# Attention logits of two groups in one call, on 64-row tiles, with a bias tile in place of two extra rows

## The chip, the cores and the metric

The kernel runs on one core of a Trainium2 chip. The time is the device time of one execution in microseconds; several executions of the kernel before are summed up by their median. TensorE (PE) multiplies, VectorE (DVE), ScalarE (ACT) and GpSimd (POOL) work on elements, SyncE (SP) issues DMAs; each engine works its own instructions off in the order in which they stand.

## The reference

256 tokens, d_model 1024, two layers. Each layer is a SwiGLU FFN (width 2816), a token mixer and another SwiGLU FFN, all with RMSNorm before and after. The first layer's mixer is an RG-LRU; the second's is an attention of 16 heads of 64 with a forget gate, and that is where the change lies. Keys, values and the cumulative sum `c` of the forget gate's logarithm are computed once from the stream after the first layer:

```python
log_f = jax.nn.log_sigmoid(hn @ w_f + b_f)
c = jnp.cumsum(log_f, axis=1).transpose(0, 2, 1)            # heads x tokens
...
q = (xq @ w_q).reshape(Bn, S, N_HEADS, HEAD_DIM).transpose(0, 2, 1, 3) * (HEAD_DIM ** -0.5)
for blk in range(S // 128):                                  # two blocks of 128 queries
    logits = einsum('bhqd,bhkd->bhqk', q[:, :, q0:end], k[:, :, :end])
    logits = logits + c[:, :, q0:end, None] - c[:, :, None, :end]
    logits = where(kpos[None, :] <= qpos[:, None], logits, -inf)
    p = softmax(logits, axis=-1)
    outs.append(einsum('bhqk,bhkd->bhqd', p, v[:, :, :end]))
return concatenate(outs) @ w_o
```

Everything is float32.

## The kernel before

*Products.* Each large product is made of three matmuls of 128x512 (L183 to L185): weights and activations are split into a high part (`whi`, `xhi`) and a low part (`wlo`, `xlo`), and high x high, low x high and high x low are summed in PSUM. Weights stream from HBM on SP's queue into five `raw` buffers; ACT rounds each to `whi` (L173), DVE subtracts it to `wlo` (L177), and nine buffers of each lie between the splits and PE.

*Order of the work.* The kernel keeps a list of items, each one a piece of weight with the work that uses it, once for token half t=0 (tokens 0 to 127) and once for t=1. `slot` does one item for one half. PE's order is written out by hand; what ACT and DVE do is put in order by a scheduler, which lets steps marked `high_priority` go first, and `keep_in_program_order` fixes the order of single instructions. `defer(n, f)` issues `f` after n further slots, `ahead(i, f)` issues it with the preparation of item i. In the attention the order stands in a string, `ATT_ORDER`: `0` and `1` are the next item for that half (first the q projections, then the output projection's eight items, which accumulate over `oh`, `ol`), and `l`, `n`, `t`, `v` with a half are the next group's logits, norm, turn (transposes) and values.

*Attention.* A group is four heads at t=0 (128 keys) and two heads at t=1 (256 keys), so 512 logits in a row, one PSUM bank; there are four groups and eight. Keys and queries are held transposed, `kT` and `qT`, one head in 66 partitions: 64 of the head, and two rows that add c: q has c and -1 there, k has 1 and c with its sign, so a matmul over 66 rows gives the logit with both terms. The two rows of q come by four POOL DMAs (L947, L948), c's row of k by one per half (L994). `heads_T` scales a product's 512 columns (L954, DVE), turns them by four transposes (L959), and copies the even heads by ACT (L962) and the odd ones by DVE (L963). `running` makes c by fp32 matmuls with a triangular matrix (L991, L992).

For each group, `logits` does one matmul per head into a PSUM bank (L1063; the `gt` banks, two of them), adds the causal mask to the last block of keys in PSUM (L1064, DVE), takes the row maxima, negated (L1066, DVE), and one exp per head from PSUM with the sum accumulated beside it (L1071, ACT). `norm` multiplies by the reciprocals of the sums (L1077, L1078, DVE). `turn` does four transposes and a copy (L1084; L1086, ACT). `values` multiplies with v in pairs of heads on two halves of the columns (L1098); after eight heads the result is split into `oh` (L1104, ACT) and `ol` (L1105, DVE), which the output projection reads.

Just ahead of the attention lies the last FFN ("ffn3" in the notes on the list), whose up items end with `prod` (L510) after `sil` (L498, ACT) and whose transposes (L525) read a reloaded `prr`. The RMSNorm's reciprocal root is computed on POOL (L198, L200).

Of the kernel before, what the change touches and what calls it, by code (L numbers as in the profile page):

```python
# [16 lines left out]
P = 128  # L17
# [9 lines left out]
HA = HD + 2  # L27
# [17 lines left out]
def trunk_kernel(ctx: ExitStack, tc: tile.TileContext, A: dict, out: bass.AP):  # L45
# [8 lines left out]
    psum = ctx.enter_context(tc.tile_pool(name="psum", bufs=1, space=bass.MemoryType.PSUM))  # L54

# [862 lines left out]
    def kv_tiles():  # L918
        lp = ctx.enter_context(tc.tile_pool(name="kv", bufs=1, reuse_waits="tile"))
        kv["kT"] = lp.tile([HA, NH, S], F32, name="kT")  # L920
        kv["v"] = [lp.tile([P, D], F32, name=f"v{t}") for t in range(2)]

        kv["lf"] = [lp.tile([P, NH + 8], F32, name=f"lf{t}")[:, :NH] for t in range(2)]
        kv["c"] = [lp.tile([NH, P], F32, name=f"c{t}") for t in range(2)]
        kv["bfb"] = lp.tile([P, NH], F32, name="bfb")
        for n in ("triu", "mone", "cmask"):
            kv[n] = lp.tile([P, P], F32, name=n)

    def kv_constants():

        keep = tc.keep_in_program_order
        triu, cm = kv["triu"], kv["cmask"]
        keep(nc.gpsimd.dma_start(kv["bfb"], A["b_fgate"].partition_broadcast(P)))
        keep(nc.gpsimd.memset(triu, -1.0))
        keep(nc.gpsimd.affine_select(out=triu, in_=triu, compare_op=ALU.is_ge, fill=0.0, base=0,
                                     pattern=[[1, P]], channel_multiplier=-1))
        keep(nc.gpsimd.memset(kv["mone"], -1.0))
        keep(nc.gpsimd.memset(cm, 0.0))
        keep(nc.gpsimd.affine_select(out=cm, in_=cm, compare_op=ALU.is_ge, fill=NEG, base=0,
                                     pattern=[[-1, P]], channel_multiplier=1))  # L940
        keep(nc.gpsimd.memset(kv["kT"][HD:HA, :, :], 1.0))

    def att_rows():

        tc.keep_in_program_order(nc.scalar.activation(warm, mhalf, AF.Exp))
        for t in range(2):
            tc.keep_in_program_order(nc.gpsimd.dma_start(att["q"][t][HD:HD + 1, :, :], kv["c"][t]))  # L947
            tc.keep_in_program_order(nc.gpsimd.dma_start(att["q"][t][HD + 1:HA, :, :], kv["mone"][:NH, :]))  # L948

    def heads_T(pool, ps, t, n, scale, dst):  # L950

        tok = pool.tile([P, 512], F32, tag="prod", name=nm("htok"), bufs=2)
# [3 lines left out]
        def turn():  # L956
# [3 lines left out]
            to = dst[:HD, 8 * n:8 * n + 8, :].rearrange("p (a two) b -> p a two b", two=2)  # L960
            with tc.high_priority():
                nc.scalar.activation(to[:, :, 0, :], tp[:HD, :].rearrange("p (a b) -> p a b", a=4), AF.Copy)  # L962
                nc.vector.tensor_copy(to[:, :, 1, :], tp[HD:, :].rearrange("p (a b) -> p a b", a=4))  # L963
        defer(2, turn)

    def post_k(n):
        return lambda t, ps: heads_T(pools["f"], ps, t, n, 1.0, kv["kT"][:, :, t * P:(t + 1) * P])
# [20 lines left out]
    def running(t):  # L988
        pc = gtbank()
        if t == 1:  # L990
            nc.tensor.matmul(pc[:NH, :P], kv["lf"][0], kv["mone"], start=True, stop=False)  # L991
        nc.tensor.matmul(pc[:NH, :P], kv["lf"][t], kv["triu"], start=t == 0, stop=True)  # L992
        nc.vector.tensor_copy(kv["c"][t], pc[:NH, :P])
        nc.gpsimd.dma_start(kv["kT"][HD + 1:HA, :, t * P:(t + 1) * P], kv["c"][t])  # L994

# [41 lines left out]
    n_ffn3 = len(items)  # L1037

# [5 lines left out]
    def att_tiles():  # L1044
        ap = pools["a"]
        att["q"] = [ap.tile([HA, NH, P], F32, name=f"qT{t}") for t in range(2)]
# [3 lines left out]
    def attention(t):  # L1050
# [4 lines left out]
        mask = kv["cmask"].unsqueeze(1).to_broadcast([P, per, P])  # L1055
# [3 lines left out]
        def logits(hg):  # L1059
            hds = range(hg * per, (hg + 1) * per)  # L1060
            ps = gtbank().rearrange("p (a b) -> p a b", a=per)
            for j, hd in enumerate(hds):
                nc.tensor.matmul(ps[:, j, :], att["q"][t][:, hd, :], kv["kT"][:, hd, :nk * P], start=True, stop=True)  # L1063
            nc.vector.tensor_tensor(ps[:, :, t * P:], ps[:, :, t * P:], mask, ALU.add)  # L1064
            mx = spool.tile([P, 4], F32, tag="mx", name=nm("mx"))
            nc.vector.tensor_reduce(mx[:, :per], ps, AX.X, ALU.max, negate=True)  # L1066
            if hds[0] % 8 == 0:
# [292 lines left out]
```

## Time and profile before

Three executions took 987.85 to 989.92 us, median 988.57. The profiled execution took 987.51 us, of which 985.8 are the span that the trace covers, at a granted TensorE clock of 0.998.

| what | before |
|---|---|
| PE busy | 978.0 us, 99% |
| DVE busy | 616.6 us, 63% |
| ACT busy | 530.1 us, 54% |
| POOL busy | 47.2 us, 5% |
| logits matmuls (L1063) | 64 records, from 734.7 to 776.3 us |
| masks (L1064) and maxima (L1066) | 12 and 12 on DVE, mean 0.51 and 0.68 us |
| exps (L1071) | 32 on ACT, and 32 reads of the accumulator at 0.20 us |
| DMA, mean | 193 GB/s |

A row of the groups' view names the line, engine, operation, the tile written and those read, the shapes and the count; then come the busy time in us and the mean of one in ns, and behind the next bar the idle time of the engine just before, with what ended it. An fp32 matmul has two records. In the order of one engine, the first number is the start and the second the length; lengths of neighbours on PE overlap, so the distance from start to start is what a step costs. A row of windows gives the stretch and its length, the busy time of PE, PEld (weight loads), DVE, ACT and POOL with counts, the granted clock, the DMA share and GB/s.

### The profile page before, as it was taken

To read this page: it belongs to the slowest core of one execution; us is meant where nothing else is said; L and a number is where in the kernel's file an instruction comes from. 1 tells how busy PE (TensorE), PEld (TensorE's weight loads), DVE (VectorE), ACT (ScalarE), POOL (GpSimd) and SP (SyncE) were. 2 spreads that over 40 slices of the span, in tenths; PEclk is the share of its full clock that TensorE was granted. 3 is DMA by queue.
4 is the path that set the end of the run, shared out by engine and by line. 5 is a ranking of instruction groups with operands and counts; after the bars stand their busy time and mean duration, and the time that the engine had idled before them with its cause. 6 is when DMAs were issued, how large, how long until landed. Compare 5 with 4: busy or idle time off the path is not lost.

```text
span 985.8 us, 13028 instructions
## 1 busy us (share of the span) xinstructions
PE 978.0 (99%) x4777; PEld 813.4 (83%) x4777; DVE 616.6 (63%) x791; ACT 530.1 (54%) x753; POOL 47.2 (5%) x92
## 2 busy tenths in 40 slices
PE   9999999999999999999999999999999999999997
PEld 6888888898978888888898888888888788888886
DVE  6666554678997555554686655554488876555542
ACT  7545443568986544443564444544366755444431
POOL 2400000100003000000100000000020000000000
PEclk9999999999999999999999999999999999999999
DMA  8787766565346877666567676665552467776631
GB/s 292 263 266 249 222 210 192 158 192 162 117 126 198 241 211 212 217 207 188 131 203 242 186 220 213 214 213 185 190 173 64 123 210 235 213 213 212 205 117 43
DMA packets 99558, 190.45 MB, mean 193 GB/s; under 512 B 12734, under 2 KB 32614, under 8 KB 99494
## 3 DMA queue, kind: packets, MB, share of 16 engines
q1 hardware_dynamic: 98054, 188.95, 61.3%
q8 instruction: 38, 0.62, 0.3%
q10 hardware_dynamic: 608, 0.53, 0.2%
q0 software_dynamic: 832, 0.12, 0.1%
q14 instruction: 26, 0.21, 0.1%
HBM read 176.95 MB, written 1.05 MB: 181 GB/s over the span
## 4 chain that ended last, share of the span: by engine, by line
PE 98%; issue 1%; DVE 1%; ACT 0%; POOL 0%; POOLq 0%; DVEq 0%; ACTq 0%
PE mm L183 29%; PE mm L185 29%; PE mm L184 28%; PE gt L761 2%; PE tr L525 1%; PE mm L1195 1%; PE gt L1063 1%; PE mm L190 1%; PE mm L191 1%; PE mm L192 1%; PE mm L1098 1%; PE tr L1084 1%; PE gt L214 1%; PE tr L127 0%; PE tr L959 0%
## 5 line engine op out<-in xcount | busy, mean ns | idle before, releaser
L177 DVE TENSOR_TENSOR wlo<-raw,whi 128x1024 fp32r<-128x1024 f32 (+5 forms) x329 | 395.3, 1207 | 268.3 <-ACT whi L173 266.1
L173 ACT ACTIVATE whi<-raw 128x1024 fp32r<-128x1024 f32 (+5 forms) x329 | 341.9, 1046 | 314.8 <-PE mm L185 260.2
L183 PE MATMUL mm<-whi,xhi 128*128 128x512 f32 (+1 forms) x768 | 301.2, 392 | 0.0
L185 PE MATMUL mm<-whi,xlo 128*128 128x512 f32 (+1 forms) x768 | 298.2, 388 | 0.3 <-DVE xlo L228 0.3
L184 PE MATMUL mm<-wlo,xhi 128*128 128x512 f32 (+1 forms) x768 | 297.9, 388 | 0.0
L185 PEld LDWEIGHTS mm<-whi,xlo 128*128 128x128 f32 x768 | 144.2, 188 | 30.7 <-DVE xlo L228 0.7
L183 PEld LDWEIGHTS mm<-whi,xhi 128*128 128x128 f32 x768 | 144.2, 188 | 29.4 <-issue 1.3
L184 PEld LDWEIGHTS mm<-wlo,xhi 128*128 128x128 f32 x768 | 144.3, 188 | 28.2 <-DVE wlo L177 0.3
L183 PE MATMUL mm<-whi,hhi 128*128 128x512 f32 x352 | 137.9, 392 | 0.0
L185 PE MATMUL mm<-whi,hlo 128*128 128x512 f32 x352 | 137.1, 389 | 0.0
L184 PE MATMUL mm<-wlo,hhi 128*128 128x512 f32 x352 | 137.0, 389 | 0.0
L185 PEld LDWEIGHTS mm<-whi,hlo 128*128 128x128 f32 x352 | 66.1, 188 | 13.9
L184 PEld LDWEIGHTS mm<-wlo,hhi 128*128 128x128 f32 x352 | 66.1, 188 | 13.3
L183 PEld LDWEIGHTS mm<-whi,hhi 128*128 128x128 f32 x352 | 66.1, 188 | 13.3
L510 DVE SCALAR_TENSOR_TENSOR prod<-mm,rstd,sil 128x512 f32<-128x512 f32 (+1 forms) x48 | 33.8, 705 | 35.2 <-PE mm L185 31.1
L498 ACT ACTIVATE sil<-mm,rstd 128x512 f32<-128x512 f32 (+1 forms) x48 | 31.2, 651 | 38.7 <-PE mm L185 34.2
L198 POOL TENSOR_SCALAR nv<-ss 128x1 f32<-128x1 f32 x22 | 9.6, 435 | 716.3 <-ACT junk L205 716.3
L529 ACT ACTIVATE hhi<-tr 128x512 fp32r<-128x512 f32 (+1 forms) x48 | 24.8, 558 | 13.8 <-PE tr L525 13.8
L205 ACT ACTIVATE junk<-mm 128x512 bf16<-128x512 f32 x24 | 14.3, 595 | 32.7 <-PE mm L185 32.6
L272 DVE TENSOR_TENSOR t<-mm,gb 128x512 f32<-128x512 f32 x24 | 16.1, 685 | 24.7 <-ACT junk L205 24.6
L530 DVE TENSOR_TENSOR hlo<-tr,hhi 128x512 fp32r<-128x512 f32 (+1 forms) x48 | 29.2, 640 | 2.6 <-ACT hhi L529 2.6
L183 PE MATMUL mm<-whi,zhi 128*128 128x340 f32 (+2 forms) x80 | 28.2, 353 | 0.0
(196 smaller groups left out, 885.8 us busy)
## 6 DMA issues: line engine op xcount, KB each, us to landing
raw<-in_ffn_w_down_dram SPq DMA_DIRECT2D x88, 512.0 KB
raw<-in_ffn_w_up_dram SPq DMA_DIRECT2D x80, 512.0 KB
raw<-in_ffn_w_gate_dram SPq DMA_DIRECT2D x78, 512.0 KB
prr<-prod SPq DMA_DIRECT2D x40, 256.0 KB
raw<-in_rg_w_in_dram SPq DMA_DIRECT2D x10, 504.0 KB
raw<-in_rg_w_out_dram SPq DMA_DIRECT2D x10, 504.0 KB
raw<-in_ffn_w_gate_dram SPq DMA_DIRECT2D x19, 256.0 KB
raw<-in_ffn_w_up_dram SPq DMA_DIRECT2D x16, 256.0 KB
```

The costliest lines, as they stand in the source:

```text
L173: up = nc.scalar.activation(hi[:parts, c:c + m], rawv[:, c:c + m], AF.Copy)
L177: nc.vector.tensor_tensor(lo[:parts, c:c + m], rawv[:, c:c + m], hi[:parts, c:c + m].bitcast(F32), ALU.subtract)
L183: nc.tensor.matmul(ps, xh, wh, start=first, stop=False)
L184: nc.tensor.matmul(ps, xh, wl, start=False, stop=False)
L185: nc.tensor.matmul(ps, xl, wh, start=False, stop=last)
L205: nc.scalar.activation(junk[:, :src.shape[1]], src, AF.Square, scale=f, accum_out=acc)
L272: nc.vector.tensor_tensor(t1[n], pf[n], gb[:, n * 512:(n + 1) * 512], ALU.mult)
L498: nc.scalar.activation(s[:, :nn], ps, AF.Silu, scale=rs[t][:, 0:1])
L510: nc.vector.scalar_tensor_tensor(pr[:, :nn], ps, rs[t][:, 0:1], s, ALU.mult, ALU.mult)
L529: nc.scalar.activation(hv, tp[:, :nn], AF.Copy)
L530: nc.vector.tensor_tensor(lv, tp[:, :nn], hv.bitcast(F32), ALU.subtract)
L761: nc.tensor.matmul(ps[j][:w, g * S:(g + 1) * S], wv[rows, o:o + w], xc[rows, k, :], start=start, stop=stop, skip_group_check=True)
```

## The change

The two extra rows go. `kT` and `qT` now hold two heads in 128 partitions, the even head in rows 0 to 63 and the odd one in rows 64 to 127, so `heads_T` needs one ACT copy of 128x512 and no DVE copy. The causal mask and the keys' part of c become a bias: for t=0 a tile `bias0` (128 queries x 16 heads x 128 keys), for t=1 a table `bias1` of 128 x 16 x 256, made in DRAM and read into SBUF as one DMA of 2 MB ahead of the attention. Both are filled by POOL DMAs that give each partition c's rows, and by a select on POOL that puts the mask's value where the key is later than the query; `bias1`'s right half goes in four parts through tiles of the `sil` buffers during the FFN before. `running` also makes `cq`, c with queries on the partitions, by more matmuls with 16 columns.

One call of `logits` now does two groups. Its heads alternate between two `gt` banks and between the upper and the lower 64 rows of PE. For each head one DVE operation (tensor_tensor_reduce, in the program two instructions: the operation and the reading of its accumulator) takes the logit, adds the bias, negates, writes to SBUF and gives the row's minimum. Two small DVE operations for each group add and subtract `cq`, so that the minimum is rounded as it would be with the query's c in it, and the exps read SBUF with scale -1. The call of the second group does nothing on its own. `ATT_ORDER` is rewritten: the calls of `l` that do the work, and the turns and values, stand at other places among the items.

```diff
--- before.py
+++ after.py
@@ -917,39 +917,63 @@
 
     def kv_tiles():
         lp = ctx.enter_context(tc.tile_pool(name="kv", bufs=1, reuse_waits="tile"))
-        kv["kT"] = lp.tile([HA, NH, S], F32, name="kT")
+        kv["kT"] = lp.tile([P, NH // 2, S], F32, name="kT")
         kv["v"] = [lp.tile([P, D], F32, name=f"v{t}") for t in range(2)]
 
         kv["lf"] = [lp.tile([P, NH + 8], F32, name=f"lf{t}")[:, :NH] for t in range(2)]
-        kv["c"] = [lp.tile([NH, P], F32, name=f"c{t}") for t in range(2)]
+        kv["cq"] = [lp.tile([P, NH], F32, name=f"cq{t}") for t in range(2)]
         kv["bfb"] = lp.tile([P, NH], F32, name="bfb")
-        for n in ("triu", "mone", "cmask"):
-            kv[n] = lp.tile([P, P], F32, name=n)
+        kv["triu"] = lp.tile([P, P], F32, name="triu")
+        kv["one"] = lp.tile([P, 32], F32, name="one")[:, :1]
+        kv["bias0"] = lp.tile([P, NH, P], F32, name="bias0")
+        kv["rows"] = dram.tile([NH, S], F32, name="crows")
+        kv["bias1"] = dram.tile([P, NH, S], F32, name="bias1d")
 
     def kv_constants():
 
         keep = tc.keep_in_program_order
-        triu, cm = kv["triu"], kv["cmask"]
+        triu = kv["triu"]
         keep(nc.gpsimd.dma_start(kv["bfb"], A["b_fgate"].partition_broadcast(P)))
-        keep(nc.gpsimd.memset(triu, -1.0))
+        keep(nc.gpsimd.memset(triu, 1.0))
         keep(nc.gpsimd.affine_select(out=triu, in_=triu, compare_op=ALU.is_ge, fill=0.0, base=0,
                                      pattern=[[1, P]], channel_multiplier=-1))
-        keep(nc.gpsimd.memset(kv["mone"], -1.0))
-        keep(nc.gpsimd.memset(cm, 0.0))
-        keep(nc.gpsimd.affine_select(out=cm, in_=cm, compare_op=ALU.is_ge, fill=NEG, base=0,
-                                     pattern=[[-1, P]], channel_multiplier=1))
-        keep(nc.gpsimd.memset(kv["kT"][HD:HA, :, :], 1.0))
+        keep(nc.gpsimd.memset(kv["one"], 1.0))
+
+    def only_earlier(v):
+
+        tc.keep_in_program_order(
+            nc.gpsimd.affine_select(out=v, in_=v, compare_op=ALU.is_ge, fill=NEG, base=0,
+                                    pattern=[[0, 4], [-1, P]], channel_multiplier=1))
+
+    def key_rows(v, h0, nh, k):
+        tc.keep_in_program_order(nc.gpsimd.dma_start(v, kv["rows"][h0:h0 + nh, k * P:(k + 1) * P].partition_broadcast(P)))
+
+    parts_of_bias = {}
+
+    def bias_rows(i):
+        def f():
+            if i == 0:
+                key_rows(kv["bias1"][:, :, :P], 0, NH, 0)
+            v = parts_of_bias[i] = pools["f"].tile([P, 512], F32, tag="sil", name=nm("bp"), bufs=2).rearrange(
+                "p (a b) -> p a b", a=4)
+            key_rows(v, 4 * i, 4, 1)
+        return f
+
+    def bias_part(i):
+        def f():
+            v = parts_of_bias.pop(i)
+            only_earlier(v)
+            tc.keep_in_program_order(nc.gpsimd.dma_start(kv["bias1"][:, 4 * i:4 * i + 4, P:], v))
+        return f
 
     def att_rows():
 
         tc.keep_in_program_order(nc.scalar.activation(warm, mhalf, AF.Exp))
-        for t in range(2):
-            tc.keep_in_program_order(nc.gpsimd.dma_start(att["q"][t][HD:HD + 1, :, :], kv["c"][t]))
-            tc.keep_in_program_order(nc.gpsimd.dma_start(att["q"][t][HD + 1:HA, :, :], kv["mone"][:NH, :]))
-
-    def heads_T(pool, ps, t, n, scale, dst):
-
-        tok = pool.tile([P, 512], F32, tag="prod", name=nm("htok"), bufs=2)
+        tc.keep_in_program_order(nc.gpsimd.dma_start(att["bias1"], kv["bias1"]))
+
+    def heads_T(pool, ps, t, n, scale, dst, tag, bufs):
+
+        tok = pool.tile([P, 512], F32, tag=tag, name=nm("htok"), bufs=bufs)
         with tc.high_priority():
             nc.vector.tensor_scalar(tok, ps, rs[t][:, 0:1], scale, ALU.mult, ALU.mult)
 
@@ -957,14 +981,12 @@
             tp = trbank()
             for j in range(4):
                 nc.tensor.transpose(tp[:, j * P:(j + 1) * P], tok[:, j * P:(j + 1) * P], ident)
-            to = dst[:HD, 8 * n:8 * n + 8, :].rearrange("p (a two) b -> p a two b", two=2)
             with tc.high_priority():
-                nc.scalar.activation(to[:, :, 0, :], tp[:HD, :].rearrange("p (a b) -> p a b", a=4), AF.Copy)
-                nc.vector.tensor_copy(to[:, :, 1, :], tp[HD:, :].rearrange("p (a b) -> p a b", a=4))
+                nc.scalar.activation(dst[:, 4 * n:4 * n + 4, :], tp.rearrange("p (a b) -> p a b", a=4), AF.Copy)
         defer(2, turn)
 
     def post_k(n):
-        return lambda t, ps: heads_T(pools["f"], ps, t, n, 1.0, kv["kT"][:, :, t * P:(t + 1) * P])
+        return lambda t, ps: heads_T(pools["f"], ps, t, n, 1.0, kv["kT"][:, :, t * P:(t + 1) * P], "prod", 2)
 
     def post_f(t, ps):
         fp = pools["f"]
@@ -986,12 +1008,23 @@
         rest()
 
     def running(t):
-        pc = gtbank()
+        pc, pq = gtbank(), gtbank()
+        one = kv["one"].to_broadcast([P, P])
         if t == 1:
-            nc.tensor.matmul(pc[:NH, :P], kv["lf"][0], kv["mone"], start=True, stop=False)
+            nc.tensor.matmul(pc[:NH, :P], kv["lf"][0], one, start=True, stop=False)
         nc.tensor.matmul(pc[:NH, :P], kv["lf"][t], kv["triu"], start=t == 0, stop=True)
-        nc.vector.tensor_copy(kv["c"][t], pc[:NH, :P])
-        nc.gpsimd.dma_start(kv["kT"][HD + 1:HA, :, t * P:(t + 1) * P], kv["c"][t])
+        if t == 1:
+            nc.tensor.matmul(pq[:, :NH], one, kv["lf"][0], start=True, stop=False)
+        nc.tensor.matmul(pq[:, :NH], kv["triu"], kv["lf"][t], start=t == 0, stop=True)
+        ct = pools["f"].tile([NH, P], F32, name=f"c{t}")
+        nc.vector.tensor_copy(ct, pc[:NH, :P])
+        nc.vector.tensor_copy(kv["cq"][t], pq[:, :NH])
+        nc.gpsimd.dma_start(kv["rows"][:, t * P:(t + 1) * P], ct)
+        if t == 0:
+            for h0 in range(0, NH, 4):
+                v = kv["bias0"][:, h0:h0 + 4, :]
+                key_rows(v, h0, 4, 0)
+                defer(30 + h0, lambda v=v: only_earlier(v))
 
     def z_x(t, k):
         return zx[t][0][:, k, :], zx[t][1][:, k, :]
@@ -1035,6 +1068,9 @@
     ffn_items(lambda: pools["f"], A["ffn1_w_gate"][1], A["ffn1_w_up"][1], A["ffn1_w_down"][1], A["ffn1_post_g"][1],
               std_dests(GI[("mix", 1)]))
     n_ffn3 = len(items)
+    for i in range(4):
+        ahead(n_ffn3 - 18 + 4 * i, bias_rows(i))
+        ahead(n_ffn3 - 15 + 4 * i, bias_part(i))
 
     items[n_ffn2:n_kv + 4] = items[n_kv:n_kv + 4] + items[n_ffn2:n_kv]
 
@@ -1043,7 +1079,8 @@
 
     def att_tiles():
         ap = pools["a"]
-        att["q"] = [ap.tile([HA, NH, P], F32, name=f"qT{t}") for t in range(2)]
+        att["q"] = [ap.tile([P, NH // 2, P], F32, name=f"qT{t}") for t in range(2)]
+        att["bias1"] = ap.tile([P, NH, S], F32, name="bias1")
         att["oh"] = [ap.tile([P, 8, P], F32R, name=f"oh{t}") for t in range(2)]
         att["ol"] = [ap.tile([P, 8, P], F32R, name=f"ol{t}") for t in range(2)]
 
@@ -1052,25 +1089,42 @@
         ap = pools["a"]
         nk = t + 1
         per = 4 // nk
-        mask = kv["cmask"].unsqueeze(1).to_broadcast([P, per, P])
+        bias = kv["bias0"] if t == 0 else att["bias1"]
+        w = nk * P
         box = {}
         G = NH // per
 
         def logits(hg):
-            hds = range(hg * per, (hg + 1) * per)
-            ps = gtbank().rearrange("p (a b) -> p a b", a=per)
-            for j, hd in enumerate(hds):
-                nc.tensor.matmul(ps[:, j, :], att["q"][t][:, hd, :], kv["kT"][:, hd, :nk * P], start=True, stop=True)
-            nc.vector.tensor_tensor(ps[:, :, t * P:], ps[:, :, t * P:], mask, ALU.add)
-            mx = spool.tile([P, 4], F32, tag="mx", name=nm("mx"))
-            nc.vector.tensor_reduce(mx[:, :per], ps, AX.X, ALU.max, negate=True)
-            if hds[0] % 8 == 0:
+            if hg % 2:
+                return
+            h0 = hg * per
+            ps = [gtbank() for _ in range(2)]
+
+            def logit(hd):
+                j = (hd - h0) // 2
+                return ps[hd % 2][:, j * w:(j + 1) * w]
+
+            for hd in range(h0, h0 + 2 * per):
+                r = slice(hd % 2 * HD, (hd % 2 + 1) * HD)
+                nc.tensor.matmul(logit(hd), att["q"][t][r, hd // 2, :], kv["kT"][r, hd // 2, :w], start=True, stop=True,
+                                 skip_group_check=True)
+            if h0 % 8 == 0:
                 box["sm"] = spool.tile([P, 8], F32, tag="sm", name=nm("sm"))
-            pe = ap.tile([P, per, nk * P], F32, tag="pe", name=nm("pe"), bufs=3)
-            for j, hd in enumerate(hds):
-                nc.scalar.activation(pe[:, j, :], ps[:, j, :], AF.Exp, bias=mx[:, j:j + 1],
-                                     accum_out=box["sm"][:, hd % 8:hd % 8 + 1])
-            box["pe", hg], box["s", hg] = pe, box["sm"][:, hds[0] % 8:hds[0] % 8 + per]
+            for g in (hg, hg + 1):
+                hds = range(g * per, (g + 1) * per)
+                mx = spool.tile([P, 8], F32, tag="mx", name=nm("mx"))
+                pe = ap.tile([P, per, w], F32, tag="pe", name=nm("pe"), bufs=3)
+                for j, hd in enumerate(hds):
+                    nc.vector.tensor_tensor_reduce(pe[:, j, :], logit(hd), bias[:, hd, :], -1.0, -NEG, ALU.add, ALU.min,
+                                                   mx[:, j:j + 1])
+                cq = kv["cq"][t][:, h0 + (g - hg) * per:h0 + (g - hg) * per + per]
+                nm_q = mx[:, 4:]
+                nc.vector.tensor_tensor(nm_q[:, :per], mx[:, :per], cq, ALU.add)
+                nc.vector.tensor_tensor(nm_q[:, :per], nm_q[:, :per], cq, ALU.subtract)
+                for j, hd in enumerate(hds):
+                    nc.scalar.activation(pe[:, j, :], pe[:, j, :], AF.Exp, bias=nm_q[:, j:j + 1], scale=-1.0,
+                                         accum_out=box["sm"][:, hd % 8:hd % 8 + 1])
+                box["pe", g], box["s", g] = pe, box["sm"][:, hds[0] % 8:hds[0] % 8 + per]
 
         def norm(hg):
             pe, sm = box["pe", hg], box["s", hg]
@@ -1107,7 +1161,7 @@
         return {c: [lambda i=i, f=f: f(i) for i in range(G)] for c, f in zip("lntv", (logits, norm, turn, values))}
 
     def post_q(n):
-        return lambda t, ps: heads_T(pools["a"], ps, t, n, HD ** -0.5, att["q"][t])
+        return lambda t, ps: heads_T(pools["a"], ps, t, n, HD ** -0.5, att["q"][t], "pT", 4)
 
     for n in range(2):
         proj_items(A["attn_w_q"][0], n * 512, 512, main_x, post_q(n))
@@ -1122,9 +1176,9 @@
     ffn_items(lambda: pools["f"], A["ffn2_w_gate"][1], A["ffn2_w_up"][1], A["ffn2_w_down"][1], A["ffn2_post_g"][1],
               lambda t: None, last=True)
 
-    ATT_ORDER = ("0 0 0 0 0 0 0 l0 0 1 n0 l0 1 t0 1 n0 1 l0 v0 t0 1 n0 l0 1 v0 t0 n0 1 l1 v0 t0 1 n1 l1 v0 0 "
-                 "n1 l1 t1 0 n1 l1 t1 0 n1 l1 v1 v1 t1 0 n1 l1 t1 0 n1 l1 v1 v1 t1 0 n1 l1 t1 0 n1 v1 v1 t1 0 "
-                 "t1 1 v1 v1 1 1 1 1 1 1 1")
+    ATT_ORDER = ("0 0 0 0 0 0 0 l0 0 1 n0 l0 1 1 t0 n0 1 l0 v0 1 t0 n0 l0 1 v0 n0 1 t0 l1 1 v0 t0 n1 l1 0 v0 "
+                 "n1 l1 t1 0 n1 l1 t1 0 n1 l1 v1 v1 t1 0 n1 l1 t1 0 n1 l1 v1 v1 t1 0 n1 l1 t1 0 n1 v1 v1 0 t1 1 "
+                 "t1 v1 1 v1 1 1 1 1 1 1")
 
 
     def half(t, i):
```

2 lines of the change are left out of this document (1 added, 1 removed).

## The prediction

> **What bounds the kernel now.** I read the page's busy times, its chain, the windows by stage, the order of PE's instructions, the groups by shape and the releasers of idle time.
>
> ```profile
> PE 978.0 (99%) x4777; PEld 813.4 (83%) x4777; DVE 616.6 (63%) x791; ACT 530.1 (54%) x753; POOL 47.2 (5%) x92
> PE 98%; issue 1%; DVE 1%; ACT 0%; POOL 0%; POOLq 0%; DVEq 0%; ACTq 0%
> ```
> ```profile
> 640.00:700.00 60.00, 60.00 (x274) 49.68 (x274) 31.67 (x32) 26.44 (x31) 0.00 (x0) 1.00 0.62 201
> 735.00:776.00 41.00, 40.99 (x263) 33.66 (x263) 34.29 (x58) 27.94 (x80) 0.00 (x0) 1.00 0.29 84
> ```
>
> PE is busy 99% and carries 98% of the chain, so a microsecond of PE work counts in full and one of DVE or ACT only where PE waits for it. The windows give, after the stretch, PE, PEld, DVE, ACT and POOL, then clock, DMA share and GB/s. From 735 to 776 us, where the logits lie, PE has no hole, but DVE is busy 34.3 of 41 us (84%): the cover there is thin. In 640–700 DVE has half its time free and the DMAs a share of 0.62.
>
> **Logits on PE.** PE's order (start, length, line; a matmul's records are two passes):
>
> ```profile
> 734.65 1.11 PE L1063 MATMUL gt<-kT,qT 66*128 66x128 f32 x8
> 735.52 0.47 PE L183 MATMUL mm<-whi,xhi 128*128 128x512 f32 x1
> 735.83 0.39 PE L184 MATMUL mm<-wlo,xhi 128*128 128x512 f32 x1
> 736.06 0.39 PE L185 MATMUL mm<-whi,xlo 128*128 128x512 f32 x1
> ...
> 753.01 1.03 PE L1063 MATMUL gt<-kT,qT 66*128 66x256 f32 x4
> 753.97 0.66 PE L1098 MATMUL mm<-pT,v 128*64 128x128 f32 x8
> 754.55 0.66 PE L1084 MATMUL tr<-ident,pe 128*128 128x128 f32 x4
> 754.97 0.47 PE L183 MATMUL mm<-whi,xhi 128*128 128x512 f32 x1
> ```
> ```profile
> 220.85 2.95 PE L761 MATMUL gt<-xc,gw 126*126 126x256 f32 x16
> 223.73 0.50 PE L183 MATMUL mm<-whi,xhi 128*128 128x512 f32 x1
> 224.07 0.39 PE L184 MATMUL mm<-wlo,xhi 128*128 128x512 f32 x1
> ```
> ```profile
> L761 PE MATMUL gt<-xc,gw x84: 376/378/479, 220.8 to 272.5; 126*126 126x256 f32 x40, 64*126 64x256 f32 x20, 62*126 62x256 f32 x20, 84*84 84x256 f32 x4
> ```
>
> A call of one group holds PE 0.87 us (734.65 to 735.52) and lengthens the next step by 0.08 (0.31 instead of 0.23): 0.95, and twelve calls 11.4 us. The new call does two groups, alternating between 64-row tiles. The gates (L761) are the nearest row for that: in five blocks of 16 passes, 8 are of 126 rows and 8 of 64 or 62. A block takes 2.88 us. Eight full passes of 256 columns are 1.74 by the first row (0.87/8 for 128, doubled), or 1.92 by the other (0.96/4); the eight half-row ones are left with 1.14 or 0.96, not 1.74, so they overlap. They have the shape of the new call for four heads and 256 keys; eight heads and 128 keys are as many columns. With 0.11 on the next matmul a call is 1.25 (1.07), six are 7.5 (6.4): **−3.9 us**, at best −5.0. I take −3.9, since the eight passes of the first row pay one entry, as the gates' do.
>
> [...]
>
> **Sums for c, and the list's switches.**
>
> ```profile
> L991 PE MATMUL gt<-mone,lf x2: 273/278/283, 529.8 to 529.9; 128*16 128x128 f32 x2
> ```
> ```profile
> 529.82 0.39 PE L991 MATMUL gt<-mone,lf 128*16 128x128 f32 x2
> 530.05 0.38 PE L992 MATMUL gt<-triu,lf 128*16 128x128 f32 x2
> ```
>
> Three more matmuls at 0.23 us are +0.7 (their stationary side is now 128 wide, at most doubling that; not under 0.3). The new list makes 18 runs of fp32 work among the weight matmuls instead of 17, and nine calls of values instead of eight: about 0.1 each, +0.3 with rounding. Steady PE work: −3.9 + 0.7 + 0.3 = **−2.9 us**.
>
> **DVE and ACT in the stage.** By shape; the mean in ns stands before the second bar, idle time and its releaser behind it:
>
> ```profile
> L177 DVE TENSOR_TENSOR wlo<-raw,whi 128x1024 fp32r<-128x1024 f32 x11 | 13.3, 1216 | 0.1
> L1078 DVE TENSOR_TENSOR pe<-pe,sm 128x512 f32<-128x512 f32 x12 | 8.2, 686 | 0.2
> L1066 DVE TENSOR_REDUCE mx<-gt 128x2 f32<-128x512 f32 x8 | 5.5, 682 | 0.0
> L1064 DVE TENSOR_TENSOR gt<-gt,cmask 128x256 f32<-128x256 f32 x8 | 3.4, 422 | 0.9 <-PE gt L1063 0.8
> L954 DVE TENSOR_SCALAR htok<-mm,rstd 128x512 f32<-128x512 f32 x4 | 3.0, 748 | 1.3 <-PE mm L185 1.3
> L1064 DVE TENSOR_TENSOR gt<-gt,cmask 128x512 f32<-128x512 f32 x4 | 2.8, 694 | 1.5 <-PE gt L1063 1.5
> L963 DVE COPY qT<-tr 64x512 f32<-64x512 f32 x4 | 2.8, 693 | 1.7 <-ACT qT L962 1.6
> L1066 DVE TENSOR_REDUCE mx<-gt 128x4 f32<-128x512 f32 x4 | 2.7, 686 | 0.1
> ```
> ```profile
> L1086 ACT ACTIVATE pT<-tr 128x512 f32<-128x512 f32 x12 | 7.1, 594 | 5.4 <-PE tr L1084 5.3
> L1071 ACT ACTIVATION_READ_ACCUMULATOR pe<-gt,mx 128x1 f32 x32 | 6.4, 202 | 0.0
> L1071 ACT ACTIVATE pe<-gt,mx 128x128 f32<-128x128 f32 x16 | 5.7, 365 | 5.0 <-DVE mx L1066 4.5 <-DVE sm L1077 0.5
> ...
> L223 ACT ACTIVATE xhi<-xg 128x512 fp32r<-128x512 f32 x2 | 1.2, 632 | 1.7 <-DVE xg L222 1.7
> ```
> ```profile
> L249 DVE SCALAR_TENSOR_TENSOR xlo<-gt,gT,xhi x16: 334/342/351, 193.6 to 205.6; 128x128 fp32r<-128x128 f32 x16
> ```
> ```profile
> L720 DVE SCALAR_TENSOR_TENSOR xc<-mm,par,xc x33: 452/475/482, 216.1 to 267.3; 126x255 f32<-126x255 f32 x10, 126x254 f32<-126x254 f32 x10, 126x253 f32<-126x253 f32 x10, 84x255 f32<-84x255 f32 x1
> ```
> ```profile
> L984 DVE TENSOR_TENSOR lf<-z,lp x2: 167/170/174, 508.5 to 524.0; 128x16 f32<-128x16 f32 x2
> ```
>
> Gone: masks 3.4 + 2.8, reduces 5.5 + 2.7, copies of q 2.8: 17.2 us (the copies of k go too, far from any wait). New: 32 fused adds with a minimum, each followed by an instruction that reads its accumulator, and 24 corrections with cq. No row shows the fused operation; nearest are L249 (0.342 for 128 columns out of PSUM) and L720 (0.475 for 255). The read costs between 0 and 0.17 (L984); I take 0.12. 16 × 0.34 + 16 × 0.475 + 32 × 0.12 + 24 × 0.17 = 20.9: DVE **+3.7 us**, 38 of 41 (93%). It decides nothing by itself, but takes the slack from the queues. Overlapped by about 0.08 as DVE's neighbours are (L1066 starts 0.6 apart), a fused pair is 0.38 or 0.51; bounds 0.30/0.43 and 0.46/0.60. ACT's 32 exps stay; they now read SBUF, which L223 (632 ns for 512 columns out of SBUF) against L1086 (594 out of PSUM) prices at 0.04 each at most, hidden in ACT's idle time.
>
> [...]
>
> **What is late next.** What matters is the latency of a group. Before, the first exp waits for one mask and one reduce, 1.1 us; now for four or five fused pairs and two corrections, 2.3 to 2.7 us at t=0, with other work between. I laid the three engines' new orders side by side with these prices. The clearest place is the second values call, counted from the start of the second new call (heads 8–15):
> PE reaches it after call 1.16, values 0.59, six matmuls 1.45, transposes 0.41, six matmuls 1.45, transposes of htok 0.44: 5.5 us.
> DVE is by then in the order: a weight split (ends about 0.8, since the norm before it ends some 0.4 ahead of the call), htok 0.7, a split 1.15, five fused pairs 1.9, correction 0.17, pair 0.38, correction 0.2: 5.3. On ACT the copy of pT for that values call stands behind the first exp of the new group: 0.35 + 0.2 + copy 0.5 gives 6.4. **PE stands 0.9 to 1.0 us.**
> Likewise at t=1, where two splits stand between the minima and the reciprocal of the fifth pair: DVE has 7.1 us of work there (4 pairs 2.0, three splits 3.4, small ones 1.0, norm 0.7) from 1.8 on; PE is there after 8.1: 0.8. The same count gives 0.1, 0.2, 0.65, 0.4, 0.6 and 1.05 at six other transposes and values. Sum **+4.8 us**; at the low price 3.0, at the high 6.5. None at all is the lower bound: splits and buffers may give more room than I see. Net −2.9 + 4.8 = +1.9.
>
> **DMAs and POOL.**
>
> ```profile
> 645.74 0.75 DVE L510 SCALAR_TENSOR_TENSOR prod<-mm,rstd,sil 128x512 f32<-128x512 f32 x1 [1.72 <-PE mm L185]
> 656.67 0.47 ACT L498 ACTIVATE sil<-mm,rstd 128x256 f32<-128x256 f32 x1 [0.30 <-PE mm L185]
> 714.39 0.30 POOL L198 TENSOR_SCALAR nv<-ss 128x1 f32<-128x1 f32 x1 [182.85 <-ACT junk L205]
> ```
> ```profile
> qT<-c POOLq DMA_DIRECT2D x2, 8.0 KB, 5.8
> ```
> ```profile
> L935 POOL TENSOR_SCALAR_AFFINE_SELECT triu<-triu x1: 990/990/990, 312.7 to 312.7; 128x128 f32<-128x128 f32 x1
> ```
>
> bias0's four DMAs and selects run from about 520 on idle POOL and are wanted at 734. bias1's four parts wait on POOL for each other: in 5.8, select 1.0 (L935, a quarter of the columns) to 4, out 5.8: 13 to 16 us each from 646.5, so to 699 to 709, before POOL is asked for a norm at 714.4. The last gate pair's sil (656.67) now waits for part 0's write, about 659.5: three microseconds of ACT's, covered by weights split ahead, but prod and its transposes follow, +0.4 on PE (0 to 2). The load of 2 MB replaces four small DMAs at 726 and is wanted at the first t=1 call near 755, where DMAs stand at 84 GB/s: nothing. heads_T's ACT copy has the columns it had. Sum +1.9 + 0.4 = **+2.3 us**.
>
> **The rivals.** (1) *The queues hold:* PE's gapless 735–776 speaks for it, since DVE at 93% still has room; then −2.9 + 0.4 = −2.5, 986.1, and the 5.0 bound makes it −4. (2) *They cancel:* 2 to 3.5 us of stalls, 988.6. (3) *bias1 is late:* if each DMA takes over 7.7 us with a select of 1.5, the parts take over 17 us each and pass 714 and hold the norm, one microsecond of PE for each beyond; six or more, 995; the 0.62 share speaks against it. (4) *The row halves do not overlap,* so the change doesn't do what it says: −3.9 goes, 994; the gates speak against it.
>
> **How the numbers follow.** The profiled execution took 987.51, 1.1 below the median of 988.57; the difference is the same on both, so 988.57 + 2.3 = 990.9. A measurement tells about 0.2%, 2 us, from no change. Forecast 0.37, (1) 0.27, (2) 0.27, (3) 0.05, (4) 0.04: faster 0.27, same 0.27, slower 0.46. Range: −3.6 (1, some gain beyond) to the high price with sil's 2, 6.5 − 2.9 + 2 = +5.6: 985.0 to 994.2; the forecast's own is 990.6 to 993.5.
>
> **What would show it.** Right: six pairs of logits calls near 1.2 us; fused pairs near 0.38 and 0.51 us; PE idle 3 to 6 us in 730–790, ended by pT or the norm. Wrong: no idle there (1), or holes near 657–664 or 714 (3).

## The result and the profile after

The changed kernel takes 985.41 us (median; 985.15 to 985.78) against 987.99 for the kernel before beside it: a ratio of 0.9975, 95% interval 0.9966 to 0.9984, so 2.5 us faster (1.6 to 3.4). The profiled execution took 985.49 us, its span is 983.8. The forecast was 990.9, slower; the time lies at the low end of the range, and the first rival, the queues hold, with 986.1, is what happened. The two profiled executions lie 2.0 us apart (987.51 and 985.49).

The page's busy times and the chain's first line of the changed kernel:

```profile
PE 975.3 (99%) x4783; PEld 808.8 (82%) x4783; DVE 610.6 (62%) x849; ACT 530.3 (54%) x753; POOL 58.2 (6%) x107
PE 95%; DVE 2%; issue 1%; ACT 1%; DMA 0%; POOL 0%; POOLq 0%; ACTq 0%; DVEq 0%
```

PE still bounds it, with 2.7 us less work. The chain now runs 3% over DVE and ACT, so the slack there is gone in places. Where the time went is read from marks in PE's order: the transposes ahead of the attention's stretch and behind it. Kernel before, then the changed one:

```profile
727.84 1.03 PE L214 MATMUL gt<-ident,h 128*128 128x128 f32 x8
788.57 1.04 PE L214 MATMUL gt<-ident,h 128*128 128x128 f32 x8
```
```profile
728.65 1.03 PE L214 MATMUL gt<-ident,h 128*128 128x128 f32 x8
786.59 1.03 PE L214 MATMUL gt<-ident,h 128*128 128x128 f32 x8
```

At the first mark the changed kernel is 0.8 us later; 0.67 of that comes where the sums for c stand, and 0.1 stands from the start of the execution on. Between 727.84 and 788.57 the kernel before needs 60.73 us, the changed one 57.94: **2.8 us less**, where the forecast had 1.2 more (steady −3.6, waits +4.8). Of PE's and DVE's work in that stretch, in the changed kernel (PE's order, then DVE's groups, then the windows):

```profile
735.23 0.40 PE L185 MATMUL mm<-whi,xlo 128*128 128x512 f32 x1
735.56 1.16 PE L1109 MATMUL gt<-kT,qT 64*128 64x128 f32 x16
736.65 0.50 PE L183 MATMUL mm<-whi,xhi 128*128 128x512 f32 x1
736.99 0.39 PE L184 MATMUL mm<-wlo,xhi 128*128 128x512 f32 x1
...
752.74 1.14 PE L1109 MATMUL gt<-kT,qT 64*128 64x256 f32 x8
753.81 0.50 PE L183 MATMUL mm<-whi,xhi 128*128 128x512 f32 x1
```
```profile
L1118 DVE CUSTOM_DVE_ANT_0 pe<-gt,bias 128x256 f32<-128x256 f32 x16 | 6.2, 418 | 0.0
L1118 DVE CUSTOM_DVE_ANT_0 pe<-gt,bias 128x128 f32<-128x128 f32 x16 | 3.8, 284 | 3.2 <-PE gt L1109 3.2
L1118 DVE DVE_READ_ACCUMULATOR2_ANT mx<- 128x1 f32 x32 | 2.6, 83 | 0.0
```
```profile
735.00:776.00 41.00, 41.00 (x285) 31.33 (x285) 32.22 (x120) 28.82 (x82) 0.00 (x0) 1.00 0.39 124
```

A call takes 1.09 us (735.56 to 736.65) or 1.07, 0.11 on the next step (0.34 instead of 0.23) and 0.10 ahead of it (0.33 from 735.23 instead of 0.23): 1.3 us where weight products stand on both sides, and 1.25 was forecast. Only two of the six calls have weight products behind them and only four have them ahead. Taken by the starts over the whole stretch, the twelve calls of the kernel before hold PE for 10.8 us and the six new ones for 6.4; with what they add to the steps beside them, 11.0 and 7.2. PE has no hole in the window (41.00 of 41), where the forecast had 4.8 us of waits. Behind the window one weight step is 0.48 us long instead of 0.23 (779.14 to 779.62), and the chain runs over DVE's L272 there, which ends at 779.57 and reads the bank of an earlier product; it is the one clear wait of PE in the stretch, 0.25 us.

DVE is busy 32.2 us, *less* than the 34.3 before, not 38. The main reason is the operation that no row of before showed: 0.284 and 0.418 us instead of the 0.342 and 0.475 taken, and its accumulator read of 0.083 us lies beside the next operation.

### The profile page after: what moved, and what is told of

It reads as the page before. It is cut to its first block, busy times and chain, and to the rows that moved or that the text cites. A ratio compares the mean times of both kernels' runs of the same rounds, so it can differ in the third digit from the quotient of the medians.

```text
span 983.8 us, 13107 instructions
## 1 busy us (share of the span) xinstructions
PE 975.3 (99%) x4783; PEld 808.8 (82%) x4783; DVE 610.6 (62%) x849; ACT 530.3 (54%) x753; POOL 58.2 (6%) x107
## 4 chain that ended last, share of the span: by engine, by line
PE 95%; DVE 2%; issue 1%; ACT 1%; DMA 0%; POOL 0%; POOLq 0%; ACTq 0%; DVEq 0%
PE mm L183 29%; PE mm L185 28%; PE mm L184 28%; PE gt L761 2%; PE tr L525 1%; PE mm L1249 1%; PE mm L190 1%; PE mm L191 1%; PE mm L192 1%; PE gt L214 1%; DVE wlo L177 1%; ACT pe L1125 0%; PE mm L1152 0%; DMA raw<-in_ffn_w_gate_dram 0%; DVE pe L1118 0%
## 5 line engine op out<-in xcount | busy, mean ns | idle before, releaser
L272 DVE TENSOR_TENSOR t<-mm,gb 128x512 f32<-128x512 f32 x24 | 16.1, 685 | 23.6 <-ACT junk L205 23.4
```

The costliest lines, as they stand in the source:

```text
L272: nc.vector.tensor_tensor(t1[n], pf[n], gb[:, n * 512:(n + 1) * 512], ALU.mult)
```

## The experiments

Ratios are to the kernel before beside each run, with 95% intervals; the changed kernel is at 0.9975, and once more, beside the last two runs, at 0.9976 (0.9967 to 0.9986; e10). What follows is mostly read from the traces, where the stretch between the two marks repeats closely: 57.94 us in the changed kernel's trace and 57.96 in e10's.

### e1: the fused minimum at the forecast's price

```diff
                     nc.vector.tensor_tensor_reduce(pe[:, j, :], logit(hd), bias[:, hd, :], -1.0, -NEG, ALU.add, ALU.min,
                                                    mx[:, j:j + 1])
+                    pad = spool.tile([P, 96], F32, tag="pad", name=nm("pad"), bufs=2)
+                    nc.vector.tensor_tensor(pad, pe[:, j, :96], pe[:, j, :96], ALU.add)
```

> The changed kernel with one more DVE operation (an add of 128x96) behind each of the 32 fused minima; nothing is left out. A fused minimum with its accumulator read took 0.21 us (128 keys) and 0.345 us (256 keys) of DVE's time in the changed kernel; the add should bring that to about 0.38 and 0.51, the prices of the prediction. Theory: the count of the waits was right and its price wrong; then PE stands 4 to 5 us in the attention stage, and the time is 4 to 5 us above the changed kernel's, some 2 us above the kernel before. Rival: the queues had more room than the count allowed, whatever the price; then the time rises by less than 1.5 us and stays below the kernel before.

Measured: 987.88 us, 0.9999 (0.9991 to 1.0008). The whole gain is gone. DVE's order, two heads and two pads:

```profile
747.62 0.28 DVE L1118 CUSTOM_DVE_ANT_0 pe<-gt,bias 128x128 f32<-128x128 f32 x1
...
747.83 0.29 DVE L1118 CUSTOM_DVE_ANT_0 pe<-gt,bias 128x128 f32<-128x128 f32 x1
...
748.04 0.42 DVE L1121 TENSOR_TENSOR pad<-pe 128x96 f32<-128x96 f32 x2
748.38 0.28 DVE L1118 CUSTOM_DVE_ANT_0 pe<-gt,bias 128x128 f32<-128x128 f32 x1
```

A fused minimum is 0.21 us from start to start, and two with two pads 0.76 (747.62 to 748.38), so 0.38 each: the forecast's price, to the hundredth. PE's order now has holes:

```profile
753.70 0.63 PE L1140 MATMUL tr<-ident,pe 128*128 128x128 f32 x4 [1.10 <-DVE pe L1134]
774.45 0.63 PE L1140 MATMUL tr<-ident,pe 128*128 128x128 f32 x4 [0.74 <-DVE sm L1133]
789.00 1.03 PE L214 MATMUL gt<-ident,h 128*128 128x128 f32 x8
```

The two waits shown are 1.8 us. The mark behind the stretch has moved from 786.59 to 789.00, of which 0.2 was there before the stretch began: 2.2 us. Neither side's number is met: the price brings back nearly half of the 4.8 us that were counted, and the rest does not come even at that price. One caution: the scheduler knows of the pads and put some exps and copies on ACT in another order, so this isn't the counted order to the last instruction.

### e2: the row halves not side by side

```diff
-            for hd in range(h0, h0 + 2 * per):
+            for hd in [*range(h0, h0 + 2 * per, 2), *range(h0 + 1, h0 + 2 * per, 2)]:
```

> The changed kernel with the heads of a call in another order: all even heads first, then all odd ones, so that matmuls of the upper and the lower 64 rows no longer stand next to each other. Nothing is left out. Theory (the gain is the overlap of the row halves): a call of 1.09 us becomes 1.9 to 2.0, six calls cost 5 us more, and the time is about 5 us above the changed kernel's. Rival (the gain is that there are six calls in place of twelve, so fewer changes between kinds of matmul): the calls stay near 1.1 to 1.3 us and the time rises by less than 1 us.

Measured: 986.84 us, 0.9991 (0.9982 to 1.0); by the marks 1.4 us in the stretch. PE's order:

```profile
735.61 1.71 PE L1109 MATMUL gt<-kT,qT 64*128 64x128 f32 x16
737.25 0.50 PE L183 MATMUL mm<-whi,xhi 128*128 128x512 f32 x1
...
753.90 1.14 PE L1109 MATMUL gt<-kT,qT 64*128 64x256 f32 x8
754.97 0.50 PE L183 MATMUL mm<-whi,xhi 128*128 128x512 f32 x1
```

With eight heads (t=0) a call grows from 1.09 to 1.64 us, so the overlap of the halves is real and worth at least 0.55 us of each such call. With four heads (t=1) it stays at 1.07: two matmuls of the upper half stand ahead of two of the lower, and they run beside each other all the same: the call's eight passes start in four pairs, 0.013 us apart, and the first two take 0.49 us together. So this edit did not take the overlap away, only part of it in two of six calls (1.1 us); a wait of 0.35 us ahead of transposes (775.39) makes up the rest of the 1.4. Neither the theory's number nor the rival's is met. The theory took for granted that matmuls which do not stand next to each other can't overlap, but here, by the pairs and the 1.07 us, PE started matmuls of one half while earlier ones of the other half were still waiting. What a call without any overlap costs was not measured.

### e3: the old list of work

```diff
-    ATT_ORDER = ("0 0 0 0 0 0 0 l0 0 1 n0 l0 1 1 t0 n0 1 l0 v0 1 t0 n0 l0 1 v0 n0 1 t0 l1 1 v0 t0 n1 l1 0 v0 "
+    ATT_ORDER = ("0 0 0 0 0 0 0 l0 0 1 n0 l0 1 t0 1 n0 1 l0 v0 t0 1 n0 l0 1 v0 t0 n0 1 l1 v0 t0 1 n1 l1 v0 0 "
...
```

> The changed kernel with the list of work of the kernel before: every second call of the logits does nothing, and turns and values stand where they stood. Nothing is left out. Theory (with a fused minimum as short as measured, the new call's latency fits either list): within 1 us of the changed kernel. Rival (the rewritten list is what keeps PE busy): 3 us or more above it, with PE waiting at the transposes or the values.

Measured: 986.31 us, 0.9988 (0.9979 to 0.9997), 0.9 us above the changed kernel in the stretch's marks. PE waits at three transposes:

```profile
741.67 0.63 PE L1138 MATMUL tr<-ident,pe 128*128 128x128 f32 x4 [0.47 <-DVE pe L1132]
751.50 0.63 PE L1138 MATMUL tr<-ident,pe 128*128 128x128 f32 x4 [0.40 <-DVE pe L1132]
778.18 0.63 PE L1138 MATMUL tr<-ident,pe 128*128 128x128 f32 x4 [0.76 <-DVE pe L1132]
```

By the marks the theory holds, just (by the ratios it is 1.3 us, with overlapping intervals): the rewritten list is worth about 0.9 of the 2.8 us, and the call alone would have been a gain with the old one.

### e4, e7 and e5: without cq, and where the tiles lie

```diff
-        if t == 1:
-            nc.tensor.matmul(pq[:, :NH], one, kv["lf"][0], start=True, stop=False)
-        nc.tensor.matmul(pq[:, :NH], kv["triu"], kv["lf"][t], start=t == 0, stop=True)
...
-                nc.vector.tensor_tensor(nm_q[:, :per], mx[:, :per], cq, ALU.add)
-                nc.vector.tensor_tensor(nm_q[:, :per], nm_q[:, :per], cq, ALU.subtract)
```

> The changed kernel without cq: its three matmuls and two copies go, and the 24 small operations that add and subtract it, so that the exps take the unrounded minimum (a softmax does not change with the shift; only the rounding of the shift is left out). The matmuls shift everything behind them by 0.67 us in the changed kernel's trace. Theory: 0.7 us from the matmuls, and what is left of waits in the attention stage (about 0.5 us) shrinks: 0.7 to 1.1 us below the changed kernel. Rival (the small operations lie on the path of each group): 1.5 us or more below.

Measured: 990.82 us, 1.0032 (1.002 to 1.0045): 5.4 us *slower* than with cq. Both theories fall. The attention's stretch gives only 0.6 of the loss (58.51 us from mark to mark, from 732.23 on); the rest lies in all stretches that read `hhi`, `hlo`, `zhi` or their like as stationary side, where a step on `hhi` and `hlo` is 0.232 us instead of 0.227. cq's tiles (128 bytes) were gone, and every tile behind them lay 128 bytes lower: `hhi` at byte 177184 of its partition instead of 177312, that is 32 instead of 160 behind a multiple of 256, as the compiled programs have it. In the kernel before, these tiles lie 160 behind one too, so the result itself does not hang on this. e7 puts that to the test alone, by a shift of 128 bytes the other way, which comes to 32 as well:

```diff
-        kv["lf"] = [lp.tile([P, NH + 8], F32, name=f"lf{t}")[:, :NH] for t in range(2)]
+        kv["lf"] = [lp.tile([P, NH + 24], F32, name=f"lf{t}")[:, :NH] for t in range(2)]
```

> The changed kernel with lf's tiles 64 bytes wider each and nothing else: each engine has the same instructions in the same order, and every tile behind lf lies 128 bytes further on. Nothing is left out. Theory (where the stationary tiles lie sets PE's rate): the matmuls that read hhi, hlo, oh and ol stand 0.232 us apart in place of 0.227, 5 us over their stretches, and the time is 4 to 6 us above the changed kernel's. Rival (the place does not matter, e4's loss came from its queues): within 0.5 us of it.

Measured: 991.09 us, 1.0032 (1.002 to 1.0045). The theory holds: the same instructions in the same order, 5.7 us slower. PE's order in e7, and in the changed kernel:

```profile
689.92 0.40 PE L183 MATMUL mm<-whi,hhi 128*128 128x512 f32 x1
...
691.79 0.40 PE L185 MATMUL mm<-whi,hlo 128*128 128x512 f32 x1
```
```profile
689.67 0.39 PE L183 MATMUL mm<-whi,hhi 128*128 128x512 f32 x1
...
691.71 0.39 PE L183 MATMUL mm<-whi,hhi 128*128 128x512 f32 x1
```

Between the first line and the last lie eight steps in e7, 1.87 us, 0.234 each; and nine in the changed kernel, 2.04 us, 0.227 each. This sample of e7 is among the longest; over 420 to 500 us the mean step on `hhi` and `hlo` is 0.232 us in e7 and 0.227 in the changed kernel. Where the stationary tile did not move, as `xhi`, or `hhi` at 140 to 200 us, it is 0.227 in both. Of these matmuls' operands only the stationary ones had moved. Nothing in the busy column tells it: PE is busy throughout in both.

e5 is e4 with lf's tiles widened by the same 64 bytes each, so that the tiles lie where they lay:

> The run without cq (e4) again, with lf's tiles 64 bytes wider each, so that every later tile lies where it lies in the changed kernel; the rounding of the shift is left out as in e4. In e4 PE's distance from matmul to matmul was 0.232 us in place of 0.227 in all stretches that read hhi, hlo and their like as stationary side (420 to 560, 660 to 730, 920 on), and these tiles had moved by 128 bytes. Theory (the place of the tiles made e4 slow): the distance is 0.227 again, and the time is 0.7 to 1.1 us below the changed kernel's, what the matmuls and small operations are worth. Rival (without cq the queues fall out of step): it stays 3 us or more above the changed kernel.

Measured: 985.38 us, 0.9977 (0.9968 to 0.9986), the changed kernel's time. The step is 0.227 again, as the theory had it, but the expected 0.7 to 1.1 us did not come. The mark ahead of the stretch is earlier by the matmuls' price, the one behind it is not, and there is a hole:

```profile
728.04 1.03 PE L214 MATMUL gt<-ident,h 128*128 128x128 f32 x8
786.51 1.03 PE L214 MATMUL gt<-ident,h 128*128 128x128 f32 x8
...
776.41 0.66 PE L1144 MATMUL mm<-pT,v 128*64 128x128 f32 x8 [0.75 <-ACT pT L1132]
```

0.61 us are won ahead (728.65 to 728.04) and 0.53 given back (58.47 us between the marks, not 57.94): the scheduler, with 24 operations less, put a weight split between two fused minima, and a copy of pT behind an exp that waits for them.

### e9 and e8: the same without that loss

e9 puts two operations in the places of the two that were gone, on other data; DVE and ACT then have the changed kernel's order in the attention.

```diff
-                nm_q = mx
+                nm_q = mx[:, 4:]
+                nc.vector.tensor_tensor(nm_q[:, :per], mx[:, :per], mx[:, :per], ALU.min)
+                nc.vector.tensor_tensor(nm_q[:, :per], nm_q[:, :per], mx[:, :per], ALU.min)
```

> The run without cq and with the tiles in their places (e5), but with two small operations for each group put back (a minimum of mx with itself, twice), so that DVE and ACT have the changed kernel's order in the attention to the last instruction; the rounding of the shift is left out. In e5 the three matmuls had brought 0.65 us by 570 us and the attention stage gave 0.53 back. Theory (the order that came with the missing operations gave it back): 0.5 to 0.8 us below the changed kernel, the whole of the matmuls. Rival (the gain is lost for another reason): within 0.3 us of it.

e8 takes e5 and moves an item:

```diff
-... t1 0 n1 v1 v1 0 t1 1 "
+... t1 0 n1 0 v1 v1 t1 1 "
```

> The run without cq and with the tiles in their places (e5), with one item of half 0 moved ahead of the two values calls at which e5's PE stood 0.75 us; the rounding of the shift is left out. Theory: the wait shrinks by about the 0.75, and the time is 0.6 to 1.2 us below the changed kernel. Rival: the next transposes, now one item nearer, wait in its place; then it stays within 0.4 us of e5.

Measured: both 984.99 us, 0.9971 (0.996 to 0.9981) and 0.9972 (0.9962 to 0.9982); the changed kernel beside them (e10) 985.41:

> The changed kernel itself once more, beside the two others: about 2.4 us below the kernel before. No theory is at stake; it gives the two others their base on the same chip.

In e9's trace the marks lie 0.8 us earlier ahead of the stretch and 0.83 behind it (0.2 of both stands from the start of the execution on):

```profile
727.84 1.04 PE L214 MATMUL gt<-ident,h 128*128 128x128 f32 x8
785.76 1.03 PE L214 MATMUL gt<-ident,h 128*128 128x128 f32 x8
```

So nothing is given back: 57.92 us between the marks. The theory holds for e9 by its trace, which gives 0.6 us beyond the start's 0.2. e8's wait at 776 is gone, and 0.38 us of wait stand at a later values call; its stretch takes 57.84 us, 0.6 less than e5's, as its theory had it. But the medians of both lie only 0.4 us below the changed kernel's, short of either theory's range, and the intervals overlap: both beat the kernel before, and that they beat the changed kernel is likely, not shown.

### e6: add and maximum apart

```diff
+                for s in range(2):
+                    j0 = (hds[0] - h0) // 2
+                    src = ps[s][:, j0 * w:(j0 + per // 2) * w].rearrange("p (a b) -> p a b", a=per // 2)
+                    nc.vector.tensor_tensor(pe[:, s::2, :], src, bias[:, hds[0] + s:hds[0] + per:2, :], ALU.add)
+                nc.vector.tensor_reduce(mx[:, :per], pe, AX.X, ALU.max, negate=True)
```

It stands in place of the loop over the fused operation, and the exps take scale 1.

> The changed kernel with the fused minimum taken apart as the kernel before had it: two adds of 128x256 and one max reduce of 128x512 for each group, from the same two banks and the same bias; nothing is left out. By the rows of the changed kernel and of the one before that is 2 x 0.34 + 0.60 = 1.28 us of DVE for a group in place of 0.84 (t=0) or 0.69 (t=1): 6.5 us more in the stage, but as a few long operations. Theory (DVE's time for a group decides): 2 to 4 us above the changed kernel, as with the padded minima. Rival (few long operations are better than many small ones): within 1 us of it or below.

Measured: 996.59 us, 1.0088 (1.0074 to 1.0102), 11 us above the changed kernel. The direction is the theory's, the size is not. PE's order and windows:

```profile
744.21 0.63 PE L1140 MATMUL tr<-ident,pe 128*128 128x128 f32 x4 [1.01 <-DVE pe L1134]
755.20 0.63 PE L1140 MATMUL tr<-ident,pe 128*128 128x128 f32 x4 [1.29 <-DVE pe L1134]
775.85 0.63 PE L1140 MATMUL tr<-ident,pe 128*128 128x128 f32 x4 [0.95 <-ACT oh L1160]
783.38 1.09 PE L1140 MATMUL tr<-ident,pe 128*128 128x128 f32 x4 [5.52 <-DVE pe L1134]
...
785.12 0.63 PE L185 MATMUL mm<-whi,ol 128*128 128x512 f32 x1
785.55 0.63 PE L183 MATMUL mm<-whi,oh 128*128 128x512 f32 x1
```
```profile
777.00:783.50 6.50, 0.98 (x5) 0.52 (x4) 6.50 (x18) 3.23 (x13) 0.00 (x0) 0.83 0.49 150
783.50:788.00 4.50, 4.50 (x20) 3.46 (x22) 0.34 (x1) 0.60 (x1) 0.00 (x0) 0.50 0.40 125
```

Four waits are 8.8 us. The last is a single one of 5.5: DVE never rests in it (6.50 of 6.50), it does adds, reduces, `ol` and weight splits that were put ahead of the norm that PE waits for. And behind it the granted clock is 0.50 for 4.5 us: matmuls stand 0.43 us apart instead of 0.23, which costs about 2.2 us more, an estimate: half of the 4.5. The waits of 0.95 to 1.29 us left the clock at 1.00 (735 to 776 and 770 to 777 us). No wait between 1.29 and 5.52 us shows in this stretch, so what such a one does to the clock isn't known from it.

## Why the prediction was wrong, step by step

- *Logits on PE, −3.9:* right. About 11.0 us became 7.2, so −3.8. The terms were a little off on both sides: 11.4 was said for the twelve calls, as if each had a weight product behind it, and 0.10 us ahead of a new call was left out. The longer step ahead of it (0.33 us from 735.23) stands ahead of a values call too (0.32 from 755.07), not ahead of transposes (0.24 from 733.40) nor of a call in the kernel before (0.23 from 734.42). Of the 0.11 behind it, 0.08 stands behind transposes of 128 rows as well (0.31 from 733.99). What makes these steps longer isn't shown.
- *Sums for c, +0.7:* right, 0.67 by the marks; two of the three (half 1, the changed kernel):

```profile
530.74 0.40 PE L1017 MATMUL gt<-lf,one 128*128 128x16 f32 x2
530.98 0.38 PE L1018 MATMUL gt<-lf,triu 128*128 128x16 f32 x2
```

- *DVE +3.7, at 93%:* wrong in sign. DVE went from 34.3 to 32.2 of 41 us. The fused pair was put at 0.38 or 0.51 us from start to start, with 0.30 and 0.43 as the low bounds; it measures 0.21 and 0.345. Two things failed: the nearest rows (L249, L720) are other operations, longer by about 0.058 us at both sizes (0.342 against 0.284, 0.475 against 0.418), and the accumulator's read, put at 0.12, takes no time of its own: its 0.083 us lie beside the next operation. The bound from below should have taken the read as free and the operations as closer together, and not lain just 0.08 under the estimate. In e6 36 longer operations in place of the 32 give DVE about 7 us more work (groups of 9.3, 5.4 and 2.7 us, where the fused operations with their reads are busy 10.1), and most of its 11 us come from one wait and the clock behind it: whether few long operations beat many small ones isn't decided by it.
- *What is late next, +4.8:* **the step that failed.** About 0.7 us is left: in the stretch the calls bring −3.8 and the list's switches were put at +0.3, and the marks say −2.8. Of the 0.7, 0.25 is the wait at 779; the rest is spread over steps that are longer by hundredths. e1, which pays the price that was taken, brings 2.2 back: that much of the step is the price of the fused operation. The rest isn't there even then. At the values call that was worked out, the changed kernel shows why, in PE's, DVE's and ACT's orders:

```profile
744.60 1.16 PE L1109 MATMUL gt<-kT,qT 64*128 64x128 f32 x16
...
750.13 0.66 PE L1152 MATMUL mm<-pT,v 128*64 128x128 f32 x8
```
```profile
745.00 0.75 DVE L978 TENSOR_SCALAR htok<-mm,rstd 128x512 f32<-128x512 f32 x1
745.66 1.22 DVE L177 TENSOR_TENSOR wlo<-raw,whi 128x1024 fp32r<-128x1024 f32 x1
746.79 0.28 DVE L1118 CUSTOM_DVE_ANT_0 pe<-gt,bias 128x128 f32<-128x128 f32 x1
...
748.13 0.16 DVE L1123 TENSOR_TENSOR mx<-mx,cq 128x4 f32<-128x4 f32 x1
```
```profile
748.32 0.40 ACT L1125 ACTIVATE pe<-pe,mx 128x128 f32<-128x128 f32 x1 [2.12 <-DVE mx L1123]
...
748.72 0.58 ACT L1140 ACTIVATE pT<-tr 128x512 f32<-128x512 f32 x1
```

  From the call's start (744.60) the split ended after 0.4, not 0.8; the fused pairs took 0.21, not 0.38; corrections and exps, counted by their length, cost less from start to start (the exp 0.40 to the copy, not 0.55). The copy ends after 4.7, not 6.4, and PE is there at 750.13, after 5.5. At the forecast's price the six pairs would add 1.0: 5.7, a wait of 0.2 where 0.9 was said. Summed lengths, taken where starts follow more closely, and a start that was too late made a wait out of a near miss here. e1 does not test this place: its scheduler put the copy (748.64) ahead of the exp (749.62), and PE has no wait there. Whether the same holds for the other seven places isn't shown, so that the part of the 4.8 us beyond e1's 2.2 is argued from one place, not measured.
- *DMAs and POOL, +0.4:* the waiting was right, the price nothing. POOL's parts end about when they were said to. The sil that had to wait starts at 658.50 us, 1.0 later than in the kernel before, counted from the marks, where three were said; that fits the landing of part 0's write (issued at 653.79, landing 3.7 to 5.0 us later). PE notices none of it: the mark at 728 us is late by the same 0.8 us as those of 572 us.

```profile
693.58 0.78 POOL L966 DMA_DIRECT2D bias1d<-bp  x1 [0.29 <-POOL bp L945]
```
```profile
bias<-bias1d POOLq DMA_DIRECT2D x1, 2048.0 KB, 10.9
bp<-crows POOLq DMA_DIRECT2D x4, 256.0 KB, 4.7
```

  The last part is out at 693.58 plus landing, 698, where 699 to 709 was said; the load of 2 MB lands 10.9 us after its issue, about 16 us before its first use (753.91).
- *The rivals:* the first was right in its mechanism, that the queues hold, and had 0.27. That its −2.5 is met to the tenth is partly luck: it had +0.4 for the DMAs, which did not come, and nothing for the 0.7 above, which did. The fourth, that the halves don't overlap, falls by e2.

## What to carry to other kernels

When a change's verdict hangs on an operation that no row shows, its price must be bounded by what its parts could overlap, and the waits behind it counted from start to start, not by lengths; a sum of near misses is otherwise a loss on paper. In a kernel whose queues are planned by a scheduler, one operation less can cost as much as it saves (e5: 0.61 us won, 0.53 given back): compare the marks ahead of and behind the stretch, not the total. Before a small tile is added or dropped, look at where the tiles behind it come to lie (e4 and e7: 5.4 and 5.7 us).

## What the hardware showed that was not expected

- A shift of 128 bytes in the place of the stationary tiles (160 to 32 behind a multiple of 256) lengthened each matmul's step on them from 0.227 us to between 0.232 and 0.234 with PE busy throughout; over the stretches concerned 5.7 us (e7), over twice the whole change. Why it does so isn't known; only these two places were tried.
- PE started matmuls of one row half ahead of earlier ones of the other half: four of 256 columns sorted by half still took 1.07 us, their passes in pairs 0.013 us apart (e2). In this, PE did not work its instructions off strictly in the order in which they stand.
- The read of DVE's accumulator (0.083 us) ran beside the next operation: fused pairs stand 0.21 us apart, less than the main operation's 0.284.
- Behind a wait of 5.5 us PE's clock was 0.50 for 4.5 us; behind waits of 1.0 and 1.3 us it stayed at 1.00 (e6).
